# Stick-breaking attention: all transfers on SyncE's queue, a fourth split tile, keys kept in the tile of their low part, paced returns

## The chip, the cores and the metric

The kernel runs on one core of one Trainium2 chip. The metric is the device time of one execution in microseconds (us). The engines are TensorE (PE), VectorE (DVE), ScalarE (ACT), GpSimd (POOL) and SyncE (SP). SP computes nothing and issues transfers; POOL issues transfers too, and in this kernel computes a little.

## The reference

A decoder trunk of two layers on 1024 tokens of width 1024 in float32: an RG-LRU block, then stick-breaking attention with 16 heads of 64, each followed by a SwiGLU network of width 2816, with RMSNorm ahead of every part. The change touches the attention alone:

```
z = jnp.einsum("bhqd,bhkd->bhqk", qb, kb).astype(jnp.float32) * scale
strict = s_idx < t_idx
log_fail = jnp.where(strict, jax.nn.log_sigmoid(-z), 0.0)
suffix = lax.cumsum(log_fail, axis=3, reverse=True) - log_fail
weights = jnp.where(strict, jnp.exp(jax.nn.log_sigmoid(z) + suffix), 0.0)
outs.append(jnp.einsum("bhqk,bhkd->bhqd", weights.astype(vb.dtype), vb))
```

The heads' outputs are then multiplied by `attn_w_o` and added to the residual.

## The kernel before, in words

All activations lie transposed, features on the 128 partitions and tokens in two halves of 512 (n = 0, 1). A float32 number is carried as a high part and the rest, so a product takes three matmuls (`mm3`, L142).

The attention works in eight pairs of heads, q = 0 to 7, and in one loop over steps u (L1860) that runs three things side by side, in an order that the code writes out by hand. Each engine executes its instructions in the order in which the loop emits them.

- *Projections* (`qkv_steps`, L1571) of the pair after the current one, two matmul groups a step. `evacuate` (L1598) takes each result out of PSUM. For queries and keys it makes a tile `two` with the high part (ACT) and the low part (DVE), and `spread` (L1634) copies `two` into the layouts that the scores need: for queries eight transfers a pair into `q`, for keys eight into `kk`. For keys the product with the norm factors first goes into a tile `t`. For values the differences of neighbours go into `t`, are split into `vx` and turned by DMA transposes into `v`.
- *Scores* (`z_part`, `z_rest`, `scan`): per head twelve chunks, eight at the diagonal and four off it. PE makes z in one of two PSUM banks, ACT's sigmoid (L1692) takes it out, DVE's scan (L1699, L1702) makes the weights of it. The four chunks off the diagonal are split into a float16 tile `wx` (L1709 ACT, L1710 DVE), and one DMA transpose each (L1713, SP) turns it into `wt`. `wx` has three buffers.
- *Weighted values* (`av_part`, L1739): twelve units a head. Units 0 to 7 use weights turned by PE (`t_part`, `t_split`), units 8 to 11 use `wt`. The result goes through `gather`, `add_v` and `parts`; for all pairs but the last ones the two parts are stored to DRAM (`store`, L1779: `odh`, `odl`, 13 tiles each), since the projections still need the tiles `xh`, `xl`.

When the last projection has read a half of `xh`, `xl`, `bring_back` (L1514) lists the stored outputs of that half, and the loop issues one return a step before the last two heads and two a step from then on (L1867 to L1869): 26 transfers of 256 KB. `out_fill` (L1801) begins the output projection (`ob`) on them.

Before the change, SP's queue in this stage holds the weight loads `raw`, the transposes of `v` and `wt`, and nothing else; POOL's queue holds `spread`, `store` and the returns, between POOL's own additions (`add_v`, L1763). An issuing engine that waits for a tile holds all that is queued behind it. Transfers on SP rotate over eight semaphores, and each waits until the one eight places ahead has landed; those on POOL do the same with eight of their own.

Of the kernel before, what the change touches and what calls it, by code (L numbers as in the profile page):

```python
# [8 lines left out]
F32 = mybir.dt.float32  # L9
F32R = mybir.dt.float32r  # L10
BF16 = mybir.dt.bfloat16
F16 = mybir.dt.float16
# [5 lines left out]
P = 128  # L18
# [4 lines left out]
NB = 512  # L23
# [11 lines left out]
def trunk(  # L35
# [21 lines left out]
    nc = tc.nc  # L57
    f32 = lambda t: t.bitcast(F32)
# [336 lines left out]
    with ExitStack() as st:  # L395
# [17 lines left out]
        two = lp.tile([P, ND], I32, name="two")  # L413
# [979 lines left out]
    def finish(h, w, R, pp, rows):  # L1393
# [78 lines left out]
    NP = HEADS // 2  # L1472
# [7 lines left out]
    od = {  # L1480
        (q, n): [dp.tile([P, NB], F32, name=f"od{x}{q}_{n}") for x in "hl"]
        for n in range(NH)
        for q in range(NP)
        if kept(q, n)
    }

    pos, obs, begun = ExitStack(), ExitStack(), {}
    with ExitStack() as st:
        ap = st.enter_context(tc.tile_pool(name="ap", bufs=1))
# [14 lines left out]
        Q, KK, VV, VT = {}, {}, {}, {}  # L1504
# [7 lines left out]
        back = []  # L1512

        def bring_back(*which):  # L1514
            for q, n in which:
                for x, dst in enumerate((xh, xl)):
                    back.append((f32(dst[q][n]), od[q, n][x]))


        def stage(task, steps=1):  # L1520
            soon.append([steps, task])
# [76 lines left out]
        def evacuate(q, which, n, ps):  # L1598
            full = lambda tag, m: [ap.tile([P, m, S], F32R, tag=tag, name=tag, bufs=4 if m == 1 else 3) for _ in range(2)]
            cs = slice(n * NB, (n + 1) * NB)  # L1600
            if which == 2:
                if n == 0:
                    VT[q] = ap.tile([P, S + 1], F32, tag="vt", name="vt", bufs=2)
                    nc.gpsimd.memset(VT[q][:, 0:1], 0.0)
                    VV[q] = ap.tile([P, 2, NT, 2, HD], F16, tag="v", name="v", bufs=2)
                t = ap.tile([P, NB], F32, tag="t", name="t", bufs=2)
                after = VT[q][:, n * NB + 1 : (n + 1) * NB + 1]
                nc.vector.scalar_tensor_tensor(after, ps, f32(sv[q]), rbc[n], op0=ALU.mult, op1=ALU.mult)
                yield
                if q == NP - 1:  # L1610
                    bring_back(*([(NP - 2, 0)] * n), *((p, n) for p in range(NP - 2)))
                nc.vector.tensor_sub(t, VT[q][:, cs], after)
                vx = ap.tile([P, 4, 2, P], F16, tag="vx", name="vx", bufs=2)
                t3 = t.rearrange("p (b c) -> p b c", b=4)

                def low():
                    nc.vector.scalar_tensor_tensor(
                        vx[:, :, 1], t3, 1 / UP, vx[:, :, 0], op0=ALU.mult, op1=ALU.subtract
                    )
                    for hx, a in enumerate((top, bot)):  # L1620
                        nc.sync.dma_start(
                            VV[q][:, hx, 4 * n : 4 * n + 4].rearrange("p b h c -> p (b h) c"),
                            vx[a].rearrange("p b h c -> p (b h c)"),
                            transpose=True,
                        )
                def high():
                    nc.scalar.activation(vx[:, :, 0], t3, AF.Copy, scale=1 / UP)
                    stage(low)

                stage(high, 2)  # L1630
                return
            two = ap.tile([P, 2, NB], F32R, tag="two", name="two", bufs=2)

            def spread():  # L1634
                for hx, (a, b) in enumerate(((top, bot), (bot, top))):
                    if which == 0:
                        nc.gpsimd.dma_start(f32(Q[q][hx])[a, cs], f32(two)[a, 0])
                        nc.gpsimd.dma_start(f32(Q[q][hx])[b, cs], f32(two)[a, 1])
                    else:
                        for half_ in (top, bot):  # L1640
                            nc.gpsimd.dma_start(f32(KK[q][hx])[half_, :, cs], f32(two)[a])

            def low():
                nc.vector.tensor_sub(two[:, 1], t, f32(two)[:, 0])
                stage(spread)

            if which == 0:
                t = ps
                if n == 0:
                    Q[q] = [x[:, 0] for x in full("q", 1)]  # L1650
                nc.scalar.copy(two[:, 0], t)
                yield
                low()
            else:
                t = ap.tile([P, NB], F32, tag="t", name="t", bufs=2)
                nc.vector.tensor_mul(t, ps, rbc[n])
                if n == 0:
                    KK[q] = full("kk", 2)
                yield

                def high():
                    nc.scalar.copy(two[:, 0], t)
                    stage(low)

                stage(high)
# [39 lines left out]

        def turn_weights(q, hx, j, ci, c0, c1, diag):
            F = W[q, hx, j, ci].rearrange("p (b c) -> p b c", c=P)
            wx = ap.tile([P, 4, 2, P], F16, tag="wx", name="wx", bufs=3)
            nc.scalar.copy(wx[:, :, 0], F)  # L1709
            nc.vector.tensor_sub(wx[:, :, 1], F, wx[:, :, 0])  # L1710
            if j == 4:
                T[q, hx] = ap.tile([P, 8, 4, P], F16, tag="wt", name="wt", bufs=2)
            nc.sync.dma_start(T[q, hx][:, :, j % 4], wx.rearrange("p b h c -> p (b h c)"), transpose=True)  # L1713
# [25 lines left out]
        def av_part(tht, q, hx, G, kb, first, last):  # L1739
            q0 = (max(kb, 4 * G) - 4 * G) * P  # L1740
            if first:
                av[0] = psO.tile([P, NB], F32, tag="o", name="av_ps")
            ps = av[0]
            if tht is None:
                tht = [T[q, hx][:, 2 * kb + x].rearrange("p j c -> p (j c)") for x in range(2)]
            for x, t in enumerate(tht):
                nc.tensor.matmul(  # L1747
                    ps[:, q0:], lhsT=VV[q][:, hx, kb], rhs=t[:, q0:], start=first and x == 0, stop=last and x == 1
                )
            if not last:  # L1750
                return
            a, b = (top, bot)[:: 1 if hx == 0 else -1]

            def gather():
                if hx == 0:
                    oo[q, G] = ap.tile([P, NB], F32, tag="oo", name="oo", bufs=2)
                o = oo[q, G]
                nc.scalar.copy(o[a], ps[b])
                nc.vector.tensor_add(o[a], ps[a], o[a])

            def add_v():
                eng = nc.vector if q >= NP - 2 else nc.gpsimd
                eng.tensor_add(oo[q, G], oo[q, G], VT[q][:, G * NB + 1 : (G + 1) * NB + 1])  # L1763

            def parts():
                o = oo[q, G]
                down = f32(av_[q])

                def both(hi, lo):
                    nc.scalar.activation(hi, o, AF.Copy, scale=down)  # L1770
                    nc.vector.scalar_tensor_tensor(lo, o, down, f32(hi), op0=ALU.mult, op1=ALU.subtract)

                if not kept(q, G):
                    both(xh[q][G], xl[q][G])
                else:
                    oh = ap.tile([P, NB], F32R, tag="oh", name="oh", bufs=1)
                    both(oh, o.bitcast(F32R))

                    def store():  # L1779
                        nc.gpsimd.dma_start(od[q, G][0], f32(oh))  # L1780
                        nc.gpsimd.dma_start(od[q, G][1], o)

                    stage(store)

            later.insert(0, gather)
            if hx == 1:
                later.extend((add_v, lambda: None, parts))
# [32 lines left out]
        with tc.manual_schedule(engines={E.PE, E.Activation, E.DVE, E.Pool, E.SP}):  # L1820
# [11 lines left out]
            def due():  # L1832
                now = soon[:]
                soon.clear()
                for steps, task in now:
                    if steps > 1:
                        stage(task, steps - 1)
                    else:
                        task()
# [11 lines left out]
            last_two, out_work = len(units) - 2 * 12, out_fill()  # L1851
# [4 lines left out]
            def turn(some):  # L1856
                for a in some:
                    turn_weights(*a)

            for u in range(-LEAD, len(units)):  # L1860
                some = chunks[c : c + 1]
# [2 lines left out]
                    for _ in range(2):  # L1864
                        next(fill, None)
                due()
                for _ in range(1 if u < last_two else 2):  # L1867
                    if back:
                        nc.gpsimd.dma_start(*back.pop(0))  # L1869
                for a in some:  # L1870
                    z_rest(z_part(*a), *a)
                    if u % 2 or u < -2:
# [6 lines left out]
                if u % 2 == 0 and 0 <= u + 2 < len(units):  # L1879
                    two = {x: t_part(*units[x]) for x in (u + 2, u + 3) if x % 12 < 8}  # L1880
# [73 lines left out]
```

## Time and profile before

| | |
|---|---|
| median of 3 runs | 2213.24 us (2211.8 to 2220.25) |
| the profiled execution | 2215.64 us |
| its span, first to last instruction | 2213.5 us |
| PE busy | 2146.3 us, 97% |
| DVE busy | 1781.0 us, 80% |
| ACT busy | 1133.3 us, 51% |
| POOL busy | 225.5 us, 10% |
| mean granted PE clock | 0.985 |
| landing, median: `kk<-two` (64, 256 KB) | 6.3 us |
| landing, median: `wt<-wx` (64 transposes) | 4.8 us |

A row of a view names line, engine, operation and tiles as out<-in. A wait is given as "engine line <- what ended it: us in total, times, longest". Issues of transfers are not counted as busy time. "Landing" is the time from the issue of a transfer to its last byte.

### The profile page before, as it was taken

How to read it: one execution, taken by the hardware profiler on the slowest of the kernel's cores; microseconds unless marked ns; L12 is line 12 of the kernel's file. 1: busy time of each engine (PE TensorE's matmuls, PEld its weight loads, DVE VectorE, ACT ScalarE, POOL GpSimd, SP SyncE). 2: the span in 40 equal slices, each digit the busy share in tenths (PEclk: the TensorE clock that was granted, in tenths of full speed). 3: DMA queues.
4: the chain of work that ended last, by engine and by line, in shares of the span. 5: the costliest groups of instructions: out<-in, count | busy, mean ns of one | idle time of the engine just before them, and what ended most of it. 6: DMA issues, size and time to landing. Idle time of an engine off the chain costs nothing.

```text
span 2213.5 us, 28166 instructions
## 1 busy us (share of the span) xinstructions
PE 2146.3 (97%) x10158; PEld 1752.4 (79%) x10158; DVE 1781.0 (80%) x2609; ACT 1133.3 (51%) x1838; POOL 225.5 (10%) x280
## 2 busy tenths in 40 slices
PE   8999999999999999999999999769999999999999
PEld 7888888888888888887766676548888888888887
DVE  7888678888888887968787887746888888888876
ACT  6576445444444554655555565534454444354556
POOL 1222020000000000011222222311000000000002
PEclk9999999999999999999999999979999999999999
DMA  6111422244446864456777866994133444487452
GB/s 230 48 48 43 161 91 74 94 151 139 154 142 216 281 201 127 131 143 124 133 141 141 152 122 124 189 165 144 57 112 112 147 153 143 156 281 244 138 154 93
DMA packets 380843, 315.46 MB, mean 143 GB/s; under 512 B 101272, under 2 KB 296992, under 8 KB 380704
## 3 DMA queue, kind: packets, MB, share of 16 engines
q1 hardware_dynamic: 368192, 274.60, 43.2%
q0 software_dynamic: 12352, 38.81, 8.3%
q8 instruction: 79, 1.29, 0.3%
q14 instruction: 60, 0.49, 0.1%
q10 hardware_dynamic: 160, 0.27, 0.0%
HBM read 184.09 MB, written 83.36 MB: 121 GB/s over the span
## 4 chain that ended last, share of the span: by engine, by line
PE 89%; DMA 7%; DVE 1%; issue 1%; ACT 1%; POOL 0%; DVEq 0%; ACTq 0%; POOLq 0%
PE p_ps L143 17%; PE p_ps L144 17%; PE p_ps L145 17%; DMA wt<-wx 7%; PE qk_ps L143 3%; PE qk_ps L144 3%; PE qk_ps L145 3%; PE a_ps L144 3%; PE a_ps L145 3%; PE a_ps L143 3%; PE ob_ps L143 2%; PE ob_ps L145 2%; PE ob_ps L144 2%; PE av_ps L1747 2%; PE z_ps L1679 1%
## 5 line engine op out<-in xcount | busy, mean ns | idle before, releaser
L143 PE MATMUL p_ps<-vh,wbh 128*128 128x512 f32 x524 | 204.9, 391 | 0.0
L144 PE MATMUL p_ps<-vl,wbh 128*128 128x512 f32 x524 | 204.5, 390 | 0.0
L145 PE MATMUL p_ps<-vh,wbl 128*128 128x512 f32 x524 | 204.0, 389 | 0.2 <-DVE wbl L726 0.2
L143 PE MATMUL p_ps<-vh,wch 128*128 128x512 f32 x524 | 204.2, 390 | 0.0
L145 PE MATMUL p_ps<-vh,wcl 128*128 128x512 f32 x524 | 204.1, 389 | 0.0
L144 PE MATMUL p_ps<-vl,wch 128*128 128x512 f32 x524 | 203.9, 389 | 0.0
L1692 ACT ACTIVATE w<-z_ps,rs 128x128 f32<-128x128 f32 (+1 forms) x192 | 109.8, 578 | 115.8 <-PE z_ps L1680 114.5
L722 ACT CAST wbh<-sb 128x1024 fp32r<-128x1024 f32 (+2 forms) x69 | 69.6, 1009 | 192.7 <-DVE sb L702 192.7
L143 PE MATMUL p_ps<-vh,wah 128*128 128x512 f32 x396 | 154.0, 389 | 0.0
L144 PE MATMUL p_ps<-vl,wah 128*128 128x512 f32 x396 | 154.0, 389 | 0.0
L145 PE MATMUL p_ps<-vh,wal 128*128 128x512 f32 x396 | 154.0, 389 | 0.0
L1699 DVE TENSOR_TENSOR_SCAN w<-w,unit 128x128 f32<-128x128 f32 (+3 forms) x128 | 104.7, 831 | 19.6 <-ACT w L1692 19.4
L218 POOL TENSOR_TENSOR acc<-acc,rbc 128x512 f32<-128x512 f32 x30 | 40.8, 1359 | 771.2 <-ACT rbc L217 771.2
L1679 PE MATMUL z_ps<-kk,q 128*128 128x256 f32 (+1 forms) x192 | 83.1, 433 | 33.7 <-ACT w L1692 33.7
L145 PEld LDWEIGHTS p_ps<-vh,wbl 128*128 128x128 f32 x524 | 98.4, 188 | 21.6 <-DVE wbl L726 0.7
L143 PE MATMUL qk_ps<-vh,whi 128*128 128x512 f32 x264 | 115.2, 436 | 0.0
L145 PEld LDWEIGHTS p_ps<-vh,wcl 128*128 128x128 f32 x524 | 98.3, 188 | 21.0 <-DVE wcl L736 0.6
L143 PEld LDWEIGHTS p_ps<-vh,wch 128*128 128x128 f32 x524 | 98.4, 188 | 20.6 <-ACT tb L1181 0.2
L144 PEld LDWEIGHTS p_ps<-vl,wch 128*128 128x128 f32 x524 | 98.4, 188 | 20.3
L143 PEld LDWEIGHTS p_ps<-vh,wbh 128*128 128x128 f32 x524 | 98.6, 188 | 19.8 <-ACT U L1181 0.4
L144 PEld LDWEIGHTS p_ps<-vl,wbh 128*128 128x128 f32 x524 | 98.6, 188 | 18.4
L145 PE MATMUL qk_ps<-vh,wlo 128*128 128x512 f32 x264 | 105.8, 401 | 0.0
(411 smaller groups left out, 5999.9 us busy)
## 6 DMA issues: line engine op xcount, KB each, us to landing
raw<-in_ffn_w_in SPq DMA_DIRECT2D x88, 512.0 KB, 4.2
vl<-pd SPq DMA_DIRECT2D x128, 256.0 KB, 3.7
pd<-U SPq DMA_DIRECT2D x90, 256.0 KB, 2.3
kk<-two POOLq DMA_DIRECT2D x64, 256.0 KB, 6.3
raw<-in_ffn_w_out SPq DMA_DIRECT2D x56, 256.0 KB, 3.6
raw<-in_attn_w_qkv SPq DMA_DIRECT2D x24, 512.0 KB, 6.1
h<-hd SPq DMA_DIRECT2D x32, 256.0 KB, 5.3
hd<-h SPq DMA_DIRECT2D x32, 256.0 KB, 2.0
```

Of the source, the lines that this page charges most:

```text
L143: nc.tensor.matmul(ps, lhsT=wh, rhs=mh, start=first, stop=False, **kw)
L144: nc.tensor.matmul(ps, lhsT=wh, rhs=ml, start=False, stop=False, **kw)
L145: nc.tensor.matmul(ps, lhsT=wl, rhs=mh, start=False, stop=last, **kw)
L218: (eng or nc.gpsimd).tensor_add(acc[n], acc[n], sq)
L722: nc.scalar.copy(self.full(self.wb), self.full(self.sb))
L1679: nc.tensor.matmul(ps[:, 0 : c1 - c0], lhsT=lhsT, rhs=KK[q][hx][:, 0, c0:c1], start=True, stop=False)
L1692: nc.scalar.activation(F, ps[:, 0:n], AF.Sigmoid, scale=rs[:, j : j + 1])
L1699: nc.vector.tensor_tensor_scan(rev, rev, unit[:, NB - n :][:, ::-1], 0.0, op0=ALU.mult, op1=ALU.add)
L1747: nc.tensor.matmul(ps[:, q0:], lhsT=VV[q][:, hx, kb], rhs=t[:, q0:], start=first and x == 0, stop=last and x == 1)
```

## The change

Four edits, all in the attention stage.

1. The copies of `spread`, the stores and the returns are issued by SP in place of POOL, at the same places of the code.
2. `wx` has four buffers in place of three.
3. For keys, the product is written into the low half of `two` itself (`t` is now that half), and the subtraction works in place. The tile `t` is left for the values, with one buffer in place of two.
4. The returns: three tiles of the second half now come ahead of the one that was stored last, and the loop issues one return a step, and two at every even step from eight steps before the last two heads on (`u >= last_two - 8`).

```diff
-                t = ap.tile([P, NB], F32, tag="t", name="t", bufs=2)
+                t = ap.tile([P, NB], F32, tag="t", name="t", bufs=1)
...
-                    bring_back(*([(NP - 2, 0)] * n), *((p, n) for p in range(NP - 2)))
+                    some = [(p, n) for p in range(NP - 2)]
+                    bring_back(*some[:3], *([(NP - 2, 0)] * n), *some[3:])
...
-                        nc.gpsimd.dma_start(f32(Q[q][hx])[a, cs], f32(two)[a, 0])
-                        nc.gpsimd.dma_start(f32(Q[q][hx])[b, cs], f32(two)[a, 1])
+                        nc.sync.dma_start(f32(Q[q][hx])[a, cs], f32(two)[a, 0])
+                        nc.sync.dma_start(f32(Q[q][hx])[b, cs], f32(two)[a, 1])
...
-                            nc.gpsimd.dma_start(f32(KK[q][hx])[half_, :, cs], f32(two)[a])
+                            nc.sync.dma_start(f32(KK[q][hx])[half_, :, cs], f32(two)[a])
...
-                t = ap.tile([P, NB], F32, tag="t", name="t", bufs=2)
+                t = f32(two)[:, 1]
...
-            wx = ap.tile([P, 4, 2, P], F16, tag="wx", name="wx", bufs=3)
+            wx = ap.tile([P, 4, 2, P], F16, tag="wx", name="wx", bufs=4)
...
-                        nc.gpsimd.dma_start(od[q, G][0], f32(oh))
-                        nc.gpsimd.dma_start(od[q, G][1], o)
+                        nc.sync.dma_start(od[q, G][0], f32(oh))
+                        nc.sync.dma_start(od[q, G][1], o)
...
-                for _ in range(1 if u < last_two else 2):
+                for _ in range(2 if u >= last_two - 8 and u % 2 == 0 else 1):
                     if back:
-                        nc.gpsimd.dma_start(*back.pop(0))
+                        nc.sync.dma_start(*back.pop(0))
```

The order of issues at two places. First a steady pair (q = 3), around the transposes of its two heads. SP's queue before (the four transposes of the even head are the x3 and the single one, those of the odd head the x4):

```order
L1713 DMA_TRANSPOSE wt<-wx 128x8x128 x3
L116 DMA raw<-in_attn_w_qkv 128x8x128
L1713 DMA_TRANSPOSE wt<-wx 128x8x128
L116 DMA raw<-in_attn_w_qkv 128x8x128
L1713 DMA_TRANSPOSE wt<-wx 128x8x128 x4
L1621 DMA_TRANSPOSE v<-vx 128x8x64 x2
```

POOL's queue before, at the same place:

```order
L1763 TENSOR_TENSOR oo<-oo,vt 128x512
L1637 DMA q<-two 64x512
L1638 DMA q<-two 64x512
L1637 DMA q<-two 64x512
L1638 DMA q<-two 64x512
L1780 DMA odh_1_7905<-oh 128x512
L1781 DMA odl_1_7906<-oo 128x512
L1641 DMA kk<-two 64x2x512 x8
```

SP's queue now (lines from L1604 on are one higher), from the second pair of those query copies on:

```order
L1638 DMA q<-two 64x512
L1639 DMA q<-two 64x512
L1714 DMA_TRANSPOSE wt<-wx 128x8x128
L1781 DMA odh_1_7905<-oh 128x512
L1782 DMA odl_1_7906<-oo 128x512
L1642 DMA kk<-two 64x2x512 x4
L116 DMA raw<-in_attn_w_qkv 128x8x128
L1714 DMA_TRANSPOSE wt<-wx 128x8x128
L1642 DMA kk<-two 64x2x512 x4
L1714 DMA_TRANSPOSE wt<-wx 128x8x128 x3
```

The fourth transpose of the even head now stands behind the raw load and the four query copies and ahead of the stores; the first transpose of the odd head stands between the two groups of key copies, its other three behind them.

Second, the end of the stage, where the returns run. POOL's queue before, around the last store (`odh_0_7897`; `vh`, `vl` and `xg` here are the tiles of `xh`, `xl`):

```order
L1869 DMA vh_3_2540<-odh_0_7889 128x512
L1869 DMA vl_3_2541<-odl_0_7890 128x512
L1780 DMA odh_0_7897<-oh 128x512
L1781 DMA odl_0_7898<-oo 128x512
L1869 DMA xg_7655<-odh_0_7891 128x512
L1869 DMA xg_7656<-odl_0_7892 128x512
L1869 DMA vh_3_2536<-odh_0_7893 128x512
```

SP's queue now, around the same store:

```order
L1870 DMA xg_7655<-odh_0_7891 128x512
L1870 DMA xg_7656<-odl_0_7892 128x512
L116 DMA raw<-in_attn_w_o 128x8x128
L1622 DMA_TRANSPOSE v<-vx 128x8x64 x2
L1781 DMA odh_0_7897<-oh 128x512
L1782 DMA odl_0_7898<-oo 128x512
L1870 DMA vh_3_2536<-odh_0_7893 128x512
L1870 DMA vl_3_2537<-odl_0_7894 128x512
L1870 DMA xg_6481<-odh_0_7895 128x512
L1714 DMA_TRANSPOSE wt<-wx 128x8x128
L1870 DMA xg_6482<-odl_0_7896 128x512
L1870 DMA vh_3_2534<-odh_1_7899 128x512
```

One more stored output comes back ahead of the last store, and the returns and the transposes of the last heads' weights now stand in one line.

## The prediction

> **What bounds the kernel now.** I read the page first, then busy time by stretches, then the waits of TensorE (PE), ScalarE (ACT) and VectorE (DVE) in the stretch that falls out, then the transfers these waits name. From the page, the busy shares and two rows of slices:
>
> ```profile
> span 2213.5 us, 28166 instructions
> PE 2146.3 (97%) x10158; PEld 1752.4 (79%) x10158; DVE 1781.0 (80%) x2609; ACT 1133.3 (51%) x1838; POOL 225.5 (10%) x280
> ...
> PE   8999999999999999999999999769999999999999
> ...
> DMA  6111422244446864456777866994133444487452
> ```
>
> PE is the bound everywhere but in one place: the 26th and 27th of the 40 slices (7 and 6 in the PE row, 1383 to 1494 us), where the DMA row stands at 9 and 9. All edits lie in the attention stage (about 965 to 1495 us), so I cut it in two: the steady stretch of the head pairs, and the end, where the attention outputs come back from DRAM. Busy time, granted clock and DMA share of the two:
>
> ```profile
> 1030.00:1405.00 375.00, 348.12 (x1751) 260.98 (x1750) 302.47 (x450) 210.85 (x415) 94.22 (x151) 0.97 0.74 137
> 1405.00:1492.00 87.00, 58.44 (x255) 39.59 (x253) 54.65 (x79) 34.80 (x70) 20.29 (x35) 0.78 0.99 170
> ```
>
> The columns are length, then PE, weight load, DVE, ACT, POOL, then clock, DMA share, GB/s. In the steady stretch PE idles 375 - 348.1 = 26.9 us, and the granted clock of 0.97 costs it another 0.03 x 375 = 11.3 us. At the end it idles 87 - 58.4 = 28.6 us at a clock of 0.78. Who is waited for, PE's waits of the steady stretch first, then those of the end:
>
> ```profile
> PE z_ps L1679 <- ACT w L1692: 14.5, 6, 3.1
> PE av_ps L1747 <- DMA wt<-wx: 10.1, 5, 2.6
> PE av_ps L1747 <- issue: 2.3, 1, 2.3
> ```
>
> ```profile
> PE z_ps L1679 <- ACT w L1692: 19.3, 4, 14.0
> PE av_ps L1747 <- DMA wt<-wx: 5.4, 2, 4.3
> ```
>
> So 12 waits make the steady 26.9 us, two for each head pair. Six (**A**, 14.5 us) come through ACT, six (**B**, 10.1 + 2.3 = 12.4 us) are for the transposed weights themselves. What ACT waits for in A, and in the 14.0 us wait of the end:
>
> ```profile
> ACT wx L1709 <- DMA wt<-wx: 35.2, 6, 6.5
> ```
>
> ```profile
> 1456.88 0.62 ACT L1709 CAST wx<-w 128x512 f16<-128x512 f32 x1 [19.70 <-DMA wt<-wx]
> ```
>
> ACT has all three split tiles wx in flight and waits for a DMA transpose to free one; behind that wait stands the sigmoid that frees PE's score bank.
>
> **The change, part by part.** *The fourth wx tile (A).* A head turns four chunks. With three tiles the fourth split waits for the first transpose to land, with four it doesn't; the tile's next use is a whole head later, half a pair (six pairs fill the 375 us). Issue to landing of the transposes of such a moment (1030 to 1048 us), and of one without other traffic (1065 to 1070 us):
>
> ```profile
> DMA to landing us min/median/max: 3.1/6.1/11.0
> ```
>
> ```profile
> DMA to landing us min/median/max: 3.1/3.1/3.1
> ```
>
> Beside POOL's four key copies they take up to 11.0 us, alone 3.1. Even 11.0 us is far below a head, so A goes: 14.5 us, and its half of the clock loss, 5.6. What is late next is DVE, below.
>
> *The queue (B).* Score keys, queries and stores leave POOL for SP, in the order in which the code issues them. In B the fourth transpose of an even head is the late one:
>
> ```profile
> 1074.16 3.21 SPq L1713 DMA_TRANSPOSE wt<-wx  x1
> ```
>
> ```profile
> 1074.50 0.57 POOL L1780 DMA_DIRECT2D odh<-oh  x1
> ```
>
> ```profile
> 1084.10 0.51 PE L1747 MATMUL av_ps<-wt,v 128*128 128x512 f16 x1 [2.07 <-DMA wt<-wx]
> ```
>
> Issued at 1074.16, it was read at 1084.10 after a wait of 2.07: some 10 us in flight, shared with a raw load ahead of it, query copies, and the stores that POOL issued after it (the first at 1074.50). In one queue the stores stand behind it; raw load and queries stand ahead. Their issue costs it 4 x 0.52 (next rows), less what overlaps. I estimate a landing 7 to 9 us after 1074.16 in place of 9.9, so most of B goes: of 12.4 + 5.6 us I keep a third in the sum.
>
> *SP's load.* The moved issues, at the durations that POOL shows, and SP's own idle time before its transposes in the steady stretch:
>
> ```profile
> L1637 POOL DMA_DIRECT2D q<-two x32: 516/523/733, 965.2 to 1382.8; - x32
> ```
>
> ```profile
> L1641 POOL DMA_DIRECT2D kk<-two x64: 587/594/660, 977.1 to 1405.3; - x64
> ...
> DMA to landing us min/median/max: 3.0/6.3/11.0
> ```
>
> ```profile
> SPq L1713 <- DVE wx L1710: 138.2, 14, 18.0
> ```
>
> In the steady stretch some 48 queries x 0.52 + 50 keys x 0.59 + 24 stores x 0.58 (estimate from the other two) = 69 us of issue go into 138 us that SP waits there for one of its groups alone. SP isn't the bound by count. By order it can be: SP now waits for the split of a query or key (its low part is DVE's) with transposes queued behind it, for which ACT's ring and PE wait. POOL's own waits for these in the steady stretch were small:
>
> ```profile
> POOL q L1638 <- DVE two L1644: 22.7, 12, 2.6
> POOL odh L1780 <- ACT oh L1770: 22.2, 6, 3.7
> ```
>
> At most 2.6 and 3.7 us, and the first stand ahead of transposes that DVE itself makes later. I cost the blocking at 0 to 2 us for each pair (nothing below zero: a wait can't bring a gain), and take it as covered by what I keep of B. POOL's 180 issues go, off the path: POOL is 10% busy.
>
> *Keys in their low part's tile, one t.* DVE writes the product into the half of two that it later overwrites: the same three instructions, no more operands. two is taken one step earlier, t has one buffer for the values alone, 16 steps apart. Zero; what hides the earlier hold is that a tile's copies land (6.3 us in the middle, above) long before its second successor is written, a block of 16 steps on; without that cover DVE would wait for such a landing.
>
> *What holds then: DVE.* Its busy time is 302.5 us of the steady 375. Its waits there, then at the end:
>
> ```profile
> DVE wx L1710 <- ACT wx L1709: 22.7, 6, 4.5
> DVE t L1656 <- PE qk_ps L145: 20.8, 6, 4.3
> DVE tl L1734 <- ACT th L1733: 13.5, 9, 1.9
> DVE w L1699 <- ACT w L1692: 13.0, 21, 1.0
> ```
>
> ```profile
> DVE wx L1710 <- ACT wx L1709: 23.4, 4, 19.9
> DVE tl L1734 <- ACT th L1733: 3.8, 3, 2.0
> DVE w L1702 <- ACT w L1692: 2.9, 2, 1.6
> ```
>
> The first two rows of the steady stretch are A and B seen from DVE; the other two, 26.5 us, are ordinary hand-overs and stay. So DVE needs 302.5 + 26.5 = 329 us, PE without waits and at full clock 348.1 - 11.3 = 336.8. The stretch can't go below 337; 38.2 us are to be had. Since DVE then has only 8 us of slack in 337, I give back a quarter (it contains the third of B): 28.5 us saved, 346.5 left.
>
> *The end.* POOL brought 26 tiles of 256 KB back while transposes ran, and stood still before a store:
>
> ```profile
> POOL odh L1780 <- ACT oh L1770: 12.6, 1, 12.6
> ```
>
> ```profile
> L1869 POOL DMA_DIRECT2D vh<-odh x8: 546/546/624, 1407.4 to 1454.3; - x8
> ...
> DMA to landing us min/median/max: 7.4/12.6/16.5
> ```
>
> The new order paces the returns (three for two units from unit 160 on, where it was one, and two from 168), puts three more pairs' tiles ahead of the one stored last, and lets transposes stand in line with them. The same size in one queue, h loads right after the stage:
>
> ```profile
> 1486.00:1498.00 12.00, 12.00 (x60) 8.57 (x59) 6.55 (x11) 4.05 (x8) 0.00 (x0) 1.00 0.92 317
> ```
>
> All that the end moved, 170 GB/s x 87 us = 14.8 MB, of which the returns are 6.8, would need 47 us at these 317 GB/s, so DMA has room if the share of 0.99 was contention. DVE then sets the length: 54.65 + 3.8 + 2.9 = 61.4 us; of its 23.4 us I drop the 19.9 and keep 3.5, plus 1.5 for a return that still comes late behind the store: 66.4. Saved: 87 - 66.4 = 20.6 us (bounds: 0, and 25.6 without the last two).
>
> **The sum.** 28.5 + 20.6 = 49.1 us off the profiled execution's 2215.6 (2.1 over its span, 2.4 over the median of the runs): 2166.5 us; in terms of the median 2164. I say 2166.
>
> **The rivals.** *B stays (0.17).* The same bytes run ahead of the fourth transpose, queries included. Then A goes (14.5 + 5.6 = 20.1) and the end gains 20.6: 2175. For it: raw load and queries were issued before 1074.16 or beside it anyway; against it: the two stores no longer are. The Trainium skill has a rule for this case ("DMA: Bandwidth & Descriptors", "Issuing engines are not separate DMA queues"): transfers of all issuing engines end on the same 16 DMA engines and interleave, and several issuers save issue time only. By that rule merging the queues takes nothing off the traffic, only the fourth tile and the pacing count, and the time is this rival's; the 11.0 against 3.1 us above agrees that the queues share the engines, but not yet that order is worth nothing.
>
> *The end is bound by the DMA engines (0.12).* For it: 0.99 over 87 us; with the same packets in one queue the end stays at 87. Against: 317 GB/s in one queue right behind, 170 in the mixture. Time: 2215.6 - 28.5 = 2187.
>
> *SP's order makes transposes late (0.10, slower).* Key copies, whose median landing is 6.3 us, go ahead of the transposes on the same queue, and each group waits a copy burst longer. It decides from the point where the fourth transpose lands more than 9.9 us after its release. Price: six pairs x 6.3 = 38 us on top of the present waits, less the end's 20.6: 2233. Against: today both finish together, so a burst done first delays the first transposes, not the last.
>
> *Nothing moves (0.06).* DVE, with its 8 us of slack, turns each wait removed into one for its own results: within 10 us of 2213. Against: the waits of A and B are 43.5 us of DVE's own idle time.
>
> **How the numbers follow.** The forecast has 0.55. It and the first two rivals run from 2147 (all 38.2 and 25.6 us gained, 2152, and some for the clock at the end) to 2198 (B stays and half the end: 2185, or 2187 with 10 us of blocking); they hold 0.84. About 0.5% (11 us) is what a measurement of this kernel can tell from no change: faster 0.84, same 0.06, slower 0.10.
>
> **What would show it.** After: no ACT wait of wx for wt; PE's av waits for wt under 5 us in the steady stretch; its length near 346; no 14 us wait at the end, about 66 us there, with DVE the densest engine. B is wrong if PE still waits some 2 us in every pair for wt; the forecast falls as a whole if SP's waits for two or oh exceed 5 us with transposes behind them.

## The result, and the profile after

The changed kernel takes 2151.22 us in the median of four runs (2150.53 to 2152.84), the kernel before, with a fourth run on the same chip, 2216.59 (2211.8 to 2220.25): a ratio of 0.9707, 95% interval 0.9683 to 0.9732. That is faster, inside the range of 2147 to 2198, and 15 us below the 2166 forecast. The profiled executions took 2151.32 and 2215.64 us, 64.3 us apart. From the page after: the busy shares, two rows of slices, and the landing of the key copies.

```profile
span 2149.3 us, 28075 instructions
...
PE 2127.2 (99%) x10158; PEld 1742.8 (81%) x10158; DVE 1778.7 (83%) x2609; ACT 1136.3 (53%) x1838; POOL 129.0 (6%) x100
...
PE   8999999999999999999999999899999999999998
...
DMA  7111422334445774536667677972234444586442
...
kk<-two SPq DMA_DIRECT2D x64, 256.0 KB, 4.5
```

The dip of PE in two slices is one digit now. For a sum I cut both programs at the same three loop steps (u = 24, 156 and 191), so that each stretch holds the same work; the equal counts behind DVE and ACT show it. Columns: length, PE, weight load, DVE, ACT, POOL, clock, DMA share, GB/s. First before, then after, the steady stretch and the end:

```profile
1064.43:1403.48 339.05, 314.50 (x1590) 236.14 (x1589) 272.55 (x407) 191.22 (x375) 85.96 (x136) 0.97 0.75 139
1403.48:1493.21 89.73, 61.17 (x268) 41.29 (x268) 56.13 (x81) 36.13 (x73) 21.70 (x37) 0.79 0.98 171
```

```profile
1061.66:1364.48 302.82, 302.82 (x1589) 230.09 (x1588) 272.59 (x407) 193.00 (x375) 27.88 (x28) 1.00 0.72 155
1364.48:1429.30 64.82, 54.69 (x268) 37.19 (x268) 54.65 (x81) 36.55 (x73) 3.65 (x4) 0.95 0.92 237
```

- Steady: PE is busy for all of 302.82 us at the full clock, and no wait of PE is left. 36.2 us are saved: 24.6 of idle time (339.05 - 314.50) and 11.7 of busy time (314.50 - 302.82), most of it the lower clock's (0.97 before, 1.00 after; 0.03 x 339 = 10.2). The stretch begins 2.8 us earlier too, where the first wait has gone: 39.0 us by its end.
- End: 89.7 to 64.8, 24.9 saved: PE's idle time went from 28.6 to 10.1 us, its busy time from 61.2 to 54.7. With the steady part 63.9 of the 64.3.
- The same end moves the same 15.3 MB (171 GB/s x 89.7 us, and 237 x 64.8) with a lower DMA share, 0.92 for 0.98.

The transposes of the weights, from 1020 to 1375 us: duration of their issue on SP (ns, minimum, median, maximum), and their landing. It was 3.1/5.6/11.6 us in the same window before. The view tells the landing of about half of the transposes; worked out for all of them from the times at which the trace's semaphores are raised, the medians are 5.7 before and 3.4 after, with the same maxima.

```profile
L1714 SPq DMA_TRANSPOSE wt<-wx x51: 1231/1263/2947, 1035.4 to 1373.4; - x51
...
DMA to landing us min/median/max: 3.1/3.4/5.9
```

PE's waits that are left, all in the end, and DVE's in the steady stretch:

```profile
PE ob L144 <- DMA vl<-odl: 2.7, 2, 2.4
PE ob L143 <- DMA vh<-odh: 2.7, 2, 2.4
PE av_ps L1748 <- DVE tl L1735: 2.2, 4, 0.8
PE av_ps L1748 <- ACT th L1734: 2.2, 2, 1.7
```

```profile
DVE tl L1735 <- ACT th L1734: 15.7, 16, 1.9
DVE w L1700 <- ACT w L1693: 10.0, 17, 0.7
DVE two L1657 <- PE qk_ps L145: 1.7, 6, 0.3
```

### The profile page after: what moved, and what is told of

Its sections match the earlier page's. It is cut to its first block, busy times and chain, and to the rows that moved or that the text cites. A ratio compares the mean times of both kernels' runs of the same rounds, so it can differ in the third digit from the quotient of the medians.

```text
span 2149.3 us, 28075 instructions
## 1 busy us (share of the span) xinstructions
PE 2127.2 (99%) x10158; PEld 1742.8 (81%) x10158; DVE 1778.7 (83%) x2609; ACT 1136.3 (53%) x1838; POOL 129.0 (6%) x100
## 5 line engine op out<-in xcount | busy, mean ns | idle before, releaser
L144 PE MATMUL qk_ps<-vl,whi 128*128 128x512 f32 x264 | 103.3, 391 | 0.0
L143 PE MATMUL p_ps<-vh,wd 128*128 128x512 f32 x254 | 99.4, 391 | 0.1
```

The costliest lines, as they stand in the source:

```text
L143: nc.tensor.matmul(ps, lhsT=wh, rhs=mh, start=first, stop=False, **kw)
L144: nc.tensor.matmul(ps, lhsT=wh, rhs=ml, start=False, stop=False, **kw)
```

## The experiments

The change held four edits, so the question is which of them paid, and by which mechanism. **The theory:** transposes are late because another queue's transfers run beside them; in one queue they wait only for what stands ahead. **Rivals:** the fourth tile does most of it; the pace of the returns does the end; order and bytes decide, not the number of queues, so that any one group of transfers could go back to POOL unharmed; DVE, not the transfers, sets the end now. All kernels compute the whole reference. Each was timed beside the kernel before on its chip. Where landings are given below for each pair of heads, they are worked out from the semaphores' times, as above, in one execution.

| kernel | built from | median us | its before | ratio, 95% |
|---|---|---|---|---|
| e1_tile | before: tile edits only | 2188.41 | 2217.01 | 0.9893 [0.9847, 0.9939] |
| e2_queue | before: queue edit only | 2158.56 | 2217.01 | 0.9752 [0.9722, 0.9782] |
| e3_three | after: three wx tiles | 2151.85 | 2217.01 | 0.9723 [0.9688, 0.9759] |
| e4_pace | before: returns' order only | 2219.67 | 2217.01 | 1.0024 [0.9996, 1.0053] |
| e5_spread_pool | after: copies on POOL | 2153.11 | 2213.62 | 0.9730 [0.9710, 0.9750] |
| e6_returns_pool | after: returns on POOL | 2163.92 | 2213.62 | 0.9781 [0.9759, 0.9802] |
| e7_returns_act | after: returns on ACT | 2158.07 | 2213.62 | 0.9758 [0.9732, 0.9783] |
| e8_early | after: returns earlier | 2150.62 | 2213.62 | 0.9719 [0.9699, 0.9739] |
| e9_stores_pool | after: stores on POOL | 2154.66 | 2217.28 | 0.9714 [0.9700, 0.9729] |
| e10_spread_pool_three | after: copies on POOL, three tiles | 2172.68 | 2217.28 | 0.9797 [0.9778, 0.9817] |
| e11_spread_stores_pool | after: copies and stores on POOL | 2167.74 | 2217.28 | 0.9772 [0.9757, 0.9787] |
| e12_small_rows_act | e7, rows of 512 B | 2155.18 | 2216.81 | 0.9723 [0.9681, 0.9765] |

### e1_tile: the tiles without the queue

```diff
-            wx = ap.tile([P, 4, 2, P], F16, tag="wx", name="wx", bufs=3)
+            wx = ap.tile([P, 4, 2, P], F16, tag="wx", name="wx", bufs=4)
```

and edit 3 (the keys' product in `two`, one `t`).

> The kernel before with four split tiles and keys kept in the tile of their low part; all transfers issued by POOL and the returns as before. Order theory (the waits B come from two queues sharing the DMA engines, A from the third tile): A goes, 14.5 us of PE wait and some 5 us at half clock, B stays at 12 us in six waits, the end gains some 5 us of its 87: 2190 to 2196 where before has 2216. Rival (the tile does it all, the queue is neutral): no wait for wt in the steady stretch, the end near 62 us: 2151 to 2160.

28.6 us faster, to just below the order theory's 2190; the four runs lie between 2181.6 and 2201.3 us. PE's waits of the steady stretch:

```profile
PE av_ps L1747 <- DMA wt<-wx: 9.1, 5, 2.7
PE av_ps L1747 <- issue: 1.5, 1, 1.5
```

The six waits A are gone, the six of B stand at 10.6 us, and the fourth transposes of the even heads still land after 8.9 to 10.4 us (9.2 to 10.3 before). At the end two waits for `wt` are left, of 13.0 and 9.3 us. So the fourth tile removes A and nothing of B, by the mechanism of the prediction.

### e2_queue: the queue without the rest

```diff
-                        nc.gpsimd.dma_start(f32(Q[q][hx])[a, cs], f32(two)[a, 0])
+                        nc.sync.dma_start(f32(Q[q][hx])[a, cs], f32(two)[a, 0])
```

and so for the other copies, the stores and the returns; three tiles, old pace.

> The kernel before with every transfer of POOL issued by SP, and nothing else: three split tiles, returns in the old order and pace. Order theory: B goes; A goes too in the most part, since the first transpose of the odd head now stands ahead of the second burst of key copies and lands 3 to 5 us after its issue in place of 11; the end gains 10 to 25 us: 2155 to 2180. Rival (the queue is neutral, transfers of all issuers share the same engines): 2211 to 2220.

58.5 us faster, nearly the whole change. PE's waits and the landing of the transposes in the steady stretch:

```profile
PE av_ps L1747 <- DMA wt<-wx: 0.8, 1, 0.8
```

```profile
DMA to landing us min/median/max: 3.1/3.3/6.4
```

B is gone, and A with it, though `wx` has three tiles: a transpose that lands within 6.4 us frees its tile before the fourth split needs it. This I hadn't seen: A needed both the late transposes and the third tile. The two savings alone add to 87 us where both edits with the pace give 65: what the tile alone buys is contained in what the queue alone buys, as the next kernel shows.

### e3_three: the changed kernel with three tiles

```diff
-            wx = ap.tile([P, 4, 2, P], F16, tag="wx", name="wx", bufs=4)
+            wx = ap.tile([P, 4, 2, P], F16, tag="wx", name="wx", bufs=3)
```

> The changed kernel with three split tiles in place of four. If one queue alone brings the first transpose in early enough, ACT waits under 1 us for a tile: 2151 to 2157. If the fourth tile is needed (A comes back, six waits of 2.4 us with half clock behind them, and part of the 14 us wait at the end): 2171 to 2180.

2151.85 us, the changed kernel's 2151.22 within the scatter. ACT waits once for a tile, 3.9 us at the end, which is more than the 1 us expected, but PE doesn't wait behind it. With one queue the fourth tile is worth nothing. Beside e2_queue on the same chip it is 6.7 us faster: that is what the returns' order and pace bring within one queue (edit 3 lies in this difference too).

### e4_pace: the order of the returns alone

```diff
-                for _ in range(1 if u < last_two else 2):
+                for _ in range(2 if u >= last_two - 8 and u % 2 == 0 else 1):
```

with the three tiles listed ahead, all on POOL.

> The kernel before with the new order and pace of the returns alone, still issued by POOL. Order theory: the steady stretch keeps A and B (26.9 us of PE wait); at the end the returns still run beside the transposes and stand behind the last store, so under 8 us go: 2208 to 2217. Rival (the pace makes the gain of the end): the end shrinks from 87 to some 65 us: 2190 to 2196.

No difference; the runs scatter from 2207.0 to 2234.3 us, and the profile is of the fastest. PE's waits over both stretches:

```profile
PE z_ps L1680 <- ACT w L1693: 34.2, 10, 16.0
PE av_ps L1748 <- DMA wt<-wx: 12.6, 6, 3.4
```

A, B and a wait of 16.0 us at the end all stand. The pace alone does nothing while the returns run in a second queue.

### e5_spread_pool: the copies back on POOL

```diff
-                        nc.sync.dma_start(f32(Q[q][hx])[a, cs], f32(two)[a, 0])
+                        nc.gpsimd.dma_start(f32(Q[q][hx])[a, cs], f32(two)[a, 0])
```

and the other query copy and the key copy alike; stores and returns stay on SP.

> The changed kernel with the query and key copies issued by POOL again; stores and returns stay on SP, four split tiles. Order theory (a transpose is late when another queue's copies run beside it): transposes land 7 to 11 us after issue beside the key bursts, A stays away because of the fourth tile, B comes back in part, since the query copies run beside the fourth transpose but the stores no longer do: waits of 0 to 1.5 us in six pairs, 2152 to 2163. Rival (B came from the stores alone): no wait for wt, 2150 to 2153.

The time lies at the low end of the theory's range, but its simple form is wrong. The transposes of the steady stretch are as slow as before, and yet PE waits for none of them:

```profile
DMA to landing us min/median/max: 3.1/6.2/11.7
```

The slow ones (9.3 to 11.7 us) are the first two of each odd head, beside the key copies; with four tiles nobody needs them soon. The fourth of an even head, B's, landed after 6.1 to 7.1 us; the one issued at 1236.8:

```profile
L1714 SPq DMA_TRANSPOSE wt<-wx x1: 2496/2496/2496, 1236.8 to 1236.8; - x1
...
DMA to landing us min/median/max: 6.9/6.9/6.9
```

So A's late transposes are those beside the key copies, and the query copies alone don't make B. The next three kernels follow this up.

### e9_stores_pool: the stores back on POOL

```diff
-                        nc.sync.dma_start(od[q, G][0], f32(oh))
+                        nc.gpsimd.dma_start(od[q, G][0], f32(oh))
```

and the second store alike.

> The changed kernel with the stores alone issued by POOL; copies and returns on SP. If the stores beside the fourth transpose are the whole of B: six waits of 1 to 2.5 us for wt with some half clock behind them, 2162 to 2170. If B needs the query copies in POOL's queue as well: no such wait, 2150 to 2154.

2154.66 us, just above the second range. The fourth transposes landed after 5.3 to 6.3 us; the one issued at 1238.1:

```profile
L1714 SPq DMA_TRANSPOSE wt<-wx x1: 2172/2172/2172, 1238.1 to 1238.1; - x1
...
DMA to landing us min/median/max: 5.8/5.8/5.8
```

PE waits three times for `wt`, 1.5 us in all and 0.8 at the longest. The stores alone make a small part of B, not B.

### e10_spread_pool_three: copies on POOL and three tiles

e5_spread_pool with the edit of e3_three.

> The changed kernel with the query and key copies issued by POOL and three split tiles; stores and returns on SP. A is then put together from its two conditions, key bursts in a second queue and a third tile that has to come free: six waits of PE for ACT's sigmoid of 1.5 to 3 us with some half clock behind them, 14 to 20 us over the run with four tiles: 2166 to 2174. If A hung on something else (the stores, or the second buffer of t): 2151 to 2155.

A is back, at 2172.68 us. PE's waits, and the transposes with who waited for them:

```profile
PE z_ps L1680 <- ACT w L1693: 12.9, 6, 2.9
```

```profile
L1714 SPq DMA_TRANSPOSE wt<-wx x48: 1231/1276/5796, 1034.2 to 1363.2; - x48
...
  ACT wx L1710: 33.7, 6
...
DMA to landing us min/median/max: 3.1/5.6/12.2
```

Six waits, one each pair, through ACT's ring. Alone neither edit costs more than 2 us (e3_three, e5_spread_pool), together 21: A has two conditions, and taking away either ends it.

### e11_spread_stores_pool: copies and stores on POOL

The edits of e5_spread_pool and e9_stores_pool together; four tiles, returns on SP.

> The changed kernel with copies and stores issued by POOL, returns on SP, four split tiles. Both candidates for B are in the second queue: the six waits for wt of the run with four tiles alone (1.2 to 2.7 us, 10.6 in all) come back, with the end as in the changed kernel: 2161 to 2168. If they don't, B hung on the returns' place or on the end, which nothing in the steady stretch can explain: 2151 to 2155.

B is back, at 2167.74 us: PE's waits, and the fourth transpose issued at 1247.2.

```profile
PE av_ps L1748 <- DMA wt<-wx: 9.9, 5, 3.0
PE av_ps L1748 <- issue: 1.5, 1, 1.5
```

```profile
L1714 SPq DMA_TRANSPOSE wt<-wx x1: 3179/3179/3179, 1247.2 to 1247.2; - x1
...
  PE av_ps L1748: 1.8, 1
DMA to landing us min/median/max: 9.6/9.6/9.6
```

Over the six pairs: 9.2 to 10.8 us with both groups beside it, 6.1 to 7.1 with the queries alone, 5.3 to 6.3 with the stores alone, 4.4 to 4.8 in the changed kernel. PE waits up to 3.0 us, not at all, up to 0.8 and not at all. The landing alone doesn't decide the wait: with the stores alone on POOL the transpose stands behind the query copies on SP, and PE waits 0.5 us for one that lands after 5.8. But the full waits of B take both groups.

### e6_returns_pool and e7_returns_act: the returns in a second queue

```diff
-                        nc.sync.dma_start(*back.pop(0))
+                        nc.gpsimd.dma_start(*back.pop(0))
```

and with `nc.scalar` in e7. In the traces, rows of these are L1870.

> The changed kernel with the returns alone issued by POOL; copies and stores stay on SP. Order theory (the end was long because returns and transposes ran from two queues at once): the steady stretch stays without waits, at the end PE waits for wt and for the returns again, 10 to 20 us of the 25 that the end gained come back: 2161 to 2172. Rival (the end was long because the returns stood behind a store on POOL): 2150 to 2155.

> The changed kernel with the returns alone issued by ACT, a queue of the same kind as SP's but a second one. If any second queue beside the transposes makes the end long: as with POOL, 2161 to 2172. If it is POOL's kind of queue that does it: 2150 to 2156, with some 12 us of issue time (26 x 0.45) on ACT, which has room there.

On POOL 12.7 us more than the changed kernel, on ACT 6.9, in between. PE's waits of the end on POOL, then on ACT:

```profile
PE av_ps L1748 <- DMA wt<-wx: 16.4, 2, 11.1
PE z_ps L1680 <- ACT w L1693: 3.7, 2, 3.1
```

```profile
PE z_ps L1680 <- ACT w L1693: 14.3, 6, 7.6
```

The landing of the transposes from 1375 to 1425 us, in the changed kernel, with POOL's queue beside and with ACT's:

```profile
DMA to landing us min/median/max: 3.0/3.6/4.5
```

```profile
DMA to landing us min/median/max: 3.1/14.8/22.3
```

```profile
DMA to landing us min/median/max: 3.0/8.3/9.1
```

These rows tell three transposes each of the seven to nine in the window; over all of them the medians are 3.6, 11.1 and 8.3 us. So the second queue itself slows them, by how much depends on which. ACT's case has a second cause in it: returns stand in ACT's own order, ahead of the sigmoids that free PE's score bank. In this trace ACT's returns and SP's transfers take turns on one set of eight semaphores, so a return, and the sigmoid behind it, is held until the transfer eight places ahead has landed, at times a transpose. ACT waits so although a sigmoid reads no `wt`:

```profile
ACT w L1693 <- DMA wt<-wx: 14.8, 3, 9.4
```

How much of the 6.9 us is this and how much the second queue, no run separates. So the rival that any one group could go back unharmed holds nearly for the copies and for the stores (1.9 and 3.4 us above the changed kernel), and not for the returns.

### e8_early: the returns earlier, the last store later

```diff
-                    stage(store)
+                    stage(store, 3 if q == NP - 2 else 1)
...
-                for _ in range(2 if u >= last_two - 8 and u % 2 == 0 else 1):
+                for _ in range(2 if u < last_two - 8 or u % 2 == 0 else 1):
```

> The changed kernel with the first returns two a step from the start (the first pair goes ahead of the fourth transpose of head 13) and the last store two steps later, behind the returns that PE needs first. The changed kernel's PE waits 2.4 us twice for returns with 3.4 us at half clock behind each. If PE sets the end: 5 to 8 us less, 2143 to 2146. If DVE sets it, as 0.95 and more of busy time around these waits suggest: 0 to 2 us less, 2149 to 2151.

2150.62 us, no difference. The waits for returns shrink from 5.4 to 2.6 us and one of 2.5 us for ACT comes in their place. So halving the waits for returns no longer shortens the end. That DVE sets its length (54.65 us busy of 64.82) is a reading of the windows, not shown by a kernel with less work for DVE; PE is as busy there (54.69).

### e12_small_rows_act: the same returns in smaller packets

What makes a second queue slow the transposes? The packets of each queue, with the share of all 16 DMA engines that they took, in e6 from 1375 to 1425 us (SP's is q1, POOL's q0) and in e7 from 1370 to 1412 (ACT's is q10):

```profile
q1 hardware_dynamic: 12273, 4.23, 51.7%
q0 software_dynamic: 1614, 5.24, 47.5%
```

```profile
q1 hardware_dynamic: 11341, 4.20, 65.0%
q10 hardware_dynamic: 2862, 5.23, 46.8%
```

The shares are those of the packets' own times; in e7 they add to 112%, so packets overlap in part, and what follows is rough. A packet of SP's took 0.517 x 50 x 16 / 12273 = 34 ns in e6, one of POOL's (3.2 KB) 0.475 x 800 / 1614 = 235 ns, one of ACT's in e7 0.468 x 672 / 2862 = 110 ns. If an engine takes a packet of each queue in turn, a transpose, whose 1024 packets of 256 B are 64 an engine (in the changed kernel, where little but transposes runs from 1064 to 1071 us, 2751 packets move 0.69 MB), waits 64 times for one of the other queue: 64 x (34 + 235) = 17.2 us beside POOL, 64 x (38 + 110) = 9.5 beside ACT, where the views' medians of these windows were 14.8 and 8.8 (11.1 and 8.8 over all transposes). To test it, the same bytes in the same queues with packets a quarter as large:

```diff
-        (q, n): [dp.tile([P, NB], F32, name=f"od{x}{q}_{n}") for x in "hl"]
+        (q, n): [dp.tile([4, P, P], F32, name=f"od{x}{q}_{n}") for x in "hl"]
...
-                    back.append((f32(dst[q][n]), od[q, n][x]))
+                    back.append((blocks(f32(dst[q][n])), od[q, n][x].rearrange("k p c -> p k c")))
```

(`blocks` is `rearrange("p (k c) -> p k c", k=4)`; the stores alike.)

> As e7_returns_act (changed kernel, returns issued by ACT), but the stored outputs lie in DRAM as four blocks of 128 columns, so that a store or return of 256 KB moves in rows of 512 B in place of 2 KB: same bytes, same queues, same issues. Packet theory: the DMA engines take one packet of each queue in turn, so a transpose's 64 packets per engine (256 KB in packets of 256 B on 16 engines) each wait for one packet of the other queue. From the windows' packet counts: 33 ns for a packet of SP's queue, 114 ns for a packet of the returns on ACT (e7), 235 ns on POOL (e6): 64 x (33 + 114) = 9.4 us against 8.8 measured, 64 x (34 + 235) = 17.2 against 14.8. With returns of 512 B a packet (some 33 to 45 ns, as the loads of 512 B rows show): 64 x (33 + 40) = about 5 us; expected median landing of wt between 1370 and 1412 us 4.5 to 6 us, PE waits on ACT under 5 us, time 2151 to 2155. Rival, a second queue in itself or the bytes beside it slow the transposes: landing stays 8 to 9 us and the time 2156 to 2161. Third possibility, four times the packets for the same bytes fill the DMA engines for longer: returns land later than e7's 5 to 6.5 us, PE waits for them at ob, time above 2161.

Packets and landing from 1370 to 1412 us, then in e7 for the same window:

```profile
q10 hardware_dynamic: 10982, 5.46, 61.7%
q1 hardware_dynamic: 12165, 4.30, 59.8%
```

```profile
DMA to landing us min/median/max: 4.0/6.1/9.0
```

```profile
DMA to landing us min/median/max: 8.3/8.8/9.1
```

The packets went from 110 to 38 ns, the median landing in these rows from 8.8 to 6.1 us. But each row tells three transposes of seven. All seven landed, in order, after 8.8, 12.4, 10.6, 9.1, 8.3, 6.8 and 8.4 us in e7, and after 9.0, 9.0, 10.0, 6.1, 4.0, 5.4 and 7.5 in e12: medians of 8.8 and 7.5, between the packet theory's 4.5 to 6 and the rival's 8 to 9. PE still waits 11.3 us for ACT, not under 5; ACT is still held in front of its returns, 8.0 us for transposes in place of 14.8. The time, 2155.18 us against 2151 to 2155, has an interval that overlaps e7's. So smaller packets point the way of the theory, in one execution each, and packet size isn't shown to be the reason. The arithmetic of one packet each in turn has the order of the three landings right but not their sizes: 17.2 for 11.1, 9.5 for 8.8, 64 x (33 + 38) = 4.5 for 7.5. POOL's packets were not varied. That a second queue slows the transposes is shown; why it does stays open.

## Why the prediction was right, and where its sizes were off

**A and the fourth tile.** The mechanism was right (e1_tile), the 20 us are there (19.6 between e10_spread_pool_three and e5_spread_pool). That the tile is needed was wrong: one queue alone ends A (e2_queue, e3_three). This cost the forecast nothing only because the change held both edits; the same reckoning for the queue alone would have kept A.

**B and the queue.** Right that B goes. The landing of the fourth transpose was put at 7 to 9 us, it is 4.4 to 4.8, and the third of B that I kept is not lost. The reason given, that the stores fall behind it, was half of it: with the queries still on POOL it lands after 6.1 to 7.1, with the stores there after 5.3 to 6.3, with both after 9.2 to 10.8.

**"I give back a quarter."** This is the step that missed, the largest mis-sized term: 28.5 us were forecast of 38.2 to be had, 39.0 came (36.2 and the 2.8 ahead of the cut). The argument was that DVE had only 8 us of slack. DVE is busy 272.6 us of the 302.8 after and waits 27.6 (15.7 + 10.0 + 1.7 and 0.2 for `wx`), so just 2.6 us are neither work nor a wait for another engine; and PE waits for it nowhere in that stretch. Here a small slack of the second engine cost nothing, and its waits for ordinary hand-overs (26.5 us counted as fixed) were in part slack themselves. The 10.5 us between 28.5 and 39.0 are most of the 15 by which the forecast was high.

**The end.** 24.9 us came for 20.6; the bound was 25.6. The terms kept were 3.5 us of DVE's wait for ACT's split and 1.5 for a late return. DVE's wait is 1.8 us in the trace after; the returns do come late twice, 2.4 us each, but as waits of PE beside DVE's work. 4.3 us of the difference. The sign given for it, DVE as the densest engine, didn't come clearly: PE is busy 54.69 us of the 64.82 and DVE 54.65.

**SP's load and blocking, and keys in their low part's tile.** Costed at nothing, and right: SP waits for `two` 4.1 us at the longest with transposes behind it, under the 5 us named, and PE for none. DVE's waits show none for a tile `t` or `two` that is still being read. Edit 3 was not tried alone.

**The rivals.** *DMA-bound end*: out, the same bytes went at 237 GB/s in place of 171. *SP's order*: out, the fourth transpose lands earlier, not later, in each of the six pairs. *Nothing moves*: out. *B stays* rested on the rule of the Trainium skill that several issuers save issue time only ("DMA: Bandwidth & Descriptors", "Issuing engines are not separate DMA queues"). As a statement on sharing the engines the trace agrees; as a rule on time it fails: e2_queue changes nothing but the issuer of 180 transfers, and with it their place in line, and gains 58.5 us. The same page of the Trainium skill has a rule that bears on it ("Queues, rings and completion order"): an engine takes packets of its queues in turn, a whole packet at a time. The landings of e6, e7 and e12 agree in order but not in size, and no run shows whether a packet of the profile is a packet of that page. I weighed the first rule and missed the second.

## What to carry to other kernels

In this kernel a short, urgent transfer (a transpose) landed two to three times as late beside the bulk of a second queue as in one queue with it, in the order of need. So try one queue, and look at the landing times of the urgent transfer with and without the other queue's bursts; 3.1 against 11 us was where this case began. And where two conditions make a wait, as with A and B, find both: removing either ends nearly all of it, and removing the second pays little more.

## What the runs showed of the hardware

- The issue of a transpose on SP itself takes longer beside a second queue: 1.23 us at the least everywhere; at the most 5.4 in the steady stretch and 8.6 at the end before, 2.9 and 2.7 in the changed kernel, 13.7 at the end with the returns on POOL (e6).
- The key copies `kk<-two` landed after 6.3 us in the median before and after 4.5 in one line with the transposes. But on POOL without the stores, still beside the transposes, they took 4.7 (e5), and 5.9 with the stores in their own queue (e11), so little of that gain comes from joining the transposes.
- POOL's queue moved packets of 3.2 KB, ACT's of 1.8 KB for the same returns, and the transposes beside them landed after 11.1 and 8.8 us in the median of all seven in each window.
